# A hybrid decode step on one core: the page table by one small load, and the sample group's attention ordered behind the first unit of the prompt's

## The chip, the cores and the metric

The kernel runs on one core of a Trainium2 chip. The metric is the device time of one execution in microseconds (us), the median of several executions. The engines are named as in the profile: PE is TensorE (its weight loads, PEld, overlap its matmuls), DVE is VectorE, ACT is ScalarE, POOL is GpSimd and SP is SyncE, which here only issues DMAs. SPq, ACTq and POOLq are the queues on which these engines issue DMAs. Each engine takes its own instructions in the order of the program.

## What is computed

One inference step of a one-layer decoder for two groups that share their weights: a prompt group (1 sequence of 1024 tokens, width 1024) and a sample group (8 sequences, one new token each, with 1024 past tokens in paged caches). Cut to what matters:

```
z        = rmsnorm(x, g_pre) @ w_in          # queries, three pairs of keys and values, gates, z_a, q_b, f_b, i_b, z_b
prompt   : attention over compressed blocks (64), over selected blocks (here all 16 of 64 tokens, causal)
           and over a window of 512; each a softmax with a linear bias of the distance; summed by gates
           HGRN2 recurrence (4 heads, 128 x 128 state) over the 1024 tokens
sample   : full_cmp = concat(cmp_cache[page_table], new)   # page_table (8, 8) int32: 8 pages of 128 tokens per sequence
           full_slc = concat(slc_cache[page_table], new)
           the same three attentions for one query per sequence, and one step of the recurrence
h        = x + rmsnorm(concat(y_a, y_b) @ w_out, g_post)
y        = h + (p @ ple_proj) * sigmoid(h @ ple_gate)
```

The outputs are y for both groups, the new key and value rows, the windows and the recurrent states.

## The kernel before, in words

The whole step is one program of 18918 instructions. Products of float32 data are made of two or three matmuls over a high and a low part (`split`, lines 50 and 51; the weights by lines 238 and 239). Nearly every matmul is issued by the helper `mm` at line 42, so the profile tells matmuls apart by their tiles. The stages follow each other in the program in this order.

1. `consts` and `load_x`: the nine tiles of x come in by SP's queue, are normed and transposed (line 218) into `xhi` and `xlo`. `load_w` (line 225 on) brings a slice of w_in in eight pieces of 128 rows into `w_raw` (3 buffers, line 233); ACT rounds each piece to `w_hi` (line 238) and DVE makes the rest `w_lo` (line 239).
2. `project`: `feat` and `tok` make the projections, one group of columns after the other, between them the recurrence (`hgrn_a`, `hgrn_b`, `hgrn_sample`). Behind the input-gate columns (`tok(C_IB, ...)`, line 335) stands `page_index` (line 336, body 645 to 658). It loads the table with eight DMAs, the i-th of which writes page i of all 8 sequences into each of 16 partitions (16 x 8 numbers), and makes `pidx[16 i + r, b] = 16 * page_table[b, i] + r`, the row numbers by which `gather` (line 660) fetches 128 rows of 8 tokens of a cache with an indirect DMA on POOL's queue. `hgrn_sample` stores its values to `v_d` (line 427) and orders the first of the eight loads behind that store; the other seven have no order.
3. `compress`, then the last projections. While the z_b columns are projected (line 420) the maxima of units 0 and 1 of the prompt's attention are made.
4. `attention` (line 618): the prompt's attention goes by 16 units (8 blocks of 128 queries in the order 5, 6, 7, 4, 3, 2, 1, 0, times 2 key-value heads). A unit is a list of steps: for each 128 keys a block (two score matmuls of 512 columns into a "ph" buffer, exponentials by ACT at line 955 into P, on the diagonal a mask by POOL at lines 958 to 962, four matmuls P times V into a "pb" buffer), the outputs of the three branches, and the store at line 995. Between the blocks of unit i stand the maxima of unit i + 2 (scores into a "pa" buffer, reductions by DVE at lines 909 to 918, the joined reduction at line 923, and `aux`, line 931, which turns the maxima by matmuls into a row of the query tile). Unit 1's maxima end with the same two steps. "ph" and "pb" have 2 buffers each in PSUM, "pa" 3, "pt" 1.
5. Beside this runs `side_work`, a generator that is advanced once every second step: `sample_attention` (line 1000) and then `finish_setup`, which loads and splits w_out. `sample_attention` sets up (query matrices Qb, Qp and Qr from small loads; masks and distances by memsets and iotas on POOL; compressed attention), then goes through the 8 sequences four times with a `yield` at each: twice over the cached selected keys, once over the window's, and once over all values. Per sequence a gather into "sg" (3 buffers), transposes at line 1125 into "pa", a split into two of the four "KT" buffers, and two products with Qr into "pt". The new keys and values `kvs` (line 1022) also take a "KT" buffer for a while.
6. `finish`: w_out, the second norm, the gate products and the outputs.

The order of the instructions on each engine is not that of the text. A planner orders them by a priority and a simulated timeline. Inside `high_priority(offset=0)` the units' steps all start from one priority, and the side work's instructions, under `high_priority(offset=600)`, come 600 ahead of it. `after(ins, first)` (line 45) adds an edge for the planner alone: `ins` is placed behind `first`, with no semaphore between them on the chip.

Of the kernel before, what the change touches and what calls it, by code (L numbers as in the profile page):

```python
# [19 lines left out]
T = 1024  # L20
# [7 lines left out]
class Kernel:  # L28
# [195 lines left out]
    def load_w(self, src, *parts):  # L224
# [4 lines left out]
        for k in range(8):  # L229
            raw = self.wpool.tile([128, 512], F32, name="w_raw", bufs=3)[:, :width]  # L230
            o = 0
            for c0, n in parts:
                dma = nc.sync.dma_start(raw[:, o:o + n], src[k * 128:(k + 1) * 128, c0:c0 + n])
                o += n
            hi = self.wpool.tile([128, 512], F32R, name="w_hi", bufs=9)[:, :width]
            lo = self.wpool.tile([128, 512], F32R, name="w_lo", bufs=9)[:, :width]
            g = self.gpre[:, k:k + 1]
            nc.scalar.activation(hi, raw, AF.Copy, scale=g)  # L238
            nc.vector.scalar_tensor_tensor(lo, raw, g, hi.bitcast(F32), op0=OP.mult, op1=OP.subtract)  # L239
            out.append((hi, lo))  # L240
# [377 lines left out]
    def attention(self, ctx):  # L618
# [3 lines left out]
        for i, u in enumerate(units):  # L622
# [3 lines left out]
            for j, f in enumerate(blocks):  # L626
                with self.tc.high_priority(offset=0):
                    f()
                while done < len(steps) * (j + 1) // len(blocks):
                    with self.tc.high_priority(offset=0):  # L630
                        steps[done]()
                    done += 1
                n += 1
                if n % 2 == 0:
                    with self.tc.high_priority(offset=600):
                        next(side, None)
# [8 lines left out]
    def page_index(self, pool):  # L645

        nc = self.nc
        pt = self.a["page_table"]
        raw = pool.tile([128, NB], I32, name="pt_raw", bufs=1)
        for i in range(8):  # L650
            dma = nc.sync.dma_start(raw[16 * i:16 * i + 16], bass.AP(tensor=pt.tensor, offset=pt.offset + i, ap=[[0, 16], [8, NB]]))
            if i == 0:
                self.pidma = dma
        lane = pool.tile([128, NB], I32, name="pt_lane", bufs=1)
        nc.gpsimd.iota(lane, pattern=[[0, NB]], base=0, channel_multiplier=1)
        nc.vector.tensor_scalar(lane, lane, 15, None, op0=OP.bitwise_and)
        self.pidx = self.cp.tile([128, NB], I32, name="pidx")
        nc.vector.scalar_tensor_tensor(self.pidx, raw, 16.0, lane, op0=OP.mult, op1=OP.add)

# [279 lines left out]
    def branches(self, qb, g, i):  # L939
# [4 lines left out]
        for br in (2, 0, 1):  # L944
            k0, k1 = (0, 0) if br == 2 else self.ranges(qb)[br]
            acc = self.ps_b.tile([128, 512], F32, name="pb").rearrange("p (h d) -> p h d", h=4)
            for kb in range(k0, k1 + 1):
                def block(br=br, kb=kb, first=kb == k0, last=kb == k1, acc=acc):
                    n = 8 * qb + 7 if br == 2 else 128
                    ks = slice(kb * 128, kb * 128 + n)  # L950
                    ps = self.ps_h.tile([128, 512], F32, name="ph")[:n].rearrange("p (h q) -> p h q", q=128)
                    self.mm(ps, KA[br, g][:, ks], QA, True, False)
                    self.mm(ps, KB[br, g][:68, ks], QB, False, True)
# [46 lines left out]
    def sample_attention(self, ctx):  # L1000
        nc, a = self.nc, self.a
        sp = self.pool(ctx, "samp", bufs=1, side="right")
        R = 64
        tpt = lambda: self.ps_t.tile([128, 512], F32, name="pt")
        Qb = sp.tile([128, NB, 8], F32, name="Qb")
        nc.gpsimd.memset(Qb, 0.0)
        Qv = Qb.rearrange("p b (g c two) -> p g two c b", g=2, two=2)
        Qs = sp.tile([128, 4, NB], F32, name="Qs")
        Ql = sp.tile([128, 4, NB], F32, name="Ql")
        nc.sync.dma_start(Qs, self.qh_d[:, :, T:].rearrange("c p b -> p c b"))  # L1010
        nc.sync.dma_start(Ql, self.ql_d[:, :, T:].rearrange("c p b -> p c b"))
        nc.vector.tensor_tensor(Qs, Qs, Ql, op=OP.add)
# [3 lines left out]
        Qp = sp.tile([128, NB, R], F32, name="Qp")  # L1016
        nc.gpsimd.memset(Qp, 0.0)
        for h in range(8):
# [3 lines left out]
        kvs = sp.tile([128, 512], F32, name="KT", bufs=4)[:NB]  # L1022
        nc.sync.dma_start(kvs, self.kvs_d[:, 256:])
        pt = tpt()
# [11 lines left out]
        gd = self.dram.tile([NB, 24], F32, name="g_d")  # L1036
        nc.sync.dma_start(gd, self.gs)
        gate = sp.tile([R, 3], F32, name="gate")
        nc.sync.dma_start(gate, gd.rearrange("b (h t) -> (b h) t", t=3))
        li = sp.tile([R, R], I32, name="li")  # L1040
        lj = sp.tile([R, R], I32, name="lj")
        nc.gpsimd.iota(li, pattern=[[0, R]], base=0, channel_multiplier=1)
        nc.gpsimd.iota(lj, pattern=[[1, R]], base=0, channel_multiplier=0)
        sl = sp.tile([R, 1], I32, name="sl")
# [35 lines left out]
        sc = sp.tile([R, 68], F32, name="sc")  # L1080
        nc.gpsimd.memset(sc, 0.0)
        nc.gpsimd.iota(sc[:, :63], pattern=[[16, 63]], base=31 - T, channel_multiplier=0, allow_small_or_imprecise_dtypes=True)
# [14 lines left out]
        bi = sp.tile([R, 16], F32, name="bi")  # L1097
        nc.gpsimd.iota(bi, pattern=[[1, 16]], base=0, channel_multiplier=0, allow_small_or_imprecise_dtypes=True)
        nc.vector.tensor_reduce(ex[:, 0:1], ps, axis=AX.X, op=OP.min)
# [33 lines left out]
        for br in range(2):  # L1133
            nj = 4 if br else 8
            s = sp.tile([R, nj, 128], F32, name=f"s{br}")
            nc.gpsimd.iota(s, pattern=[[1, nj], [nj, 128]], base=-128 * nj, channel_multiplier=0,
                           allow_small_or_imprecise_dtypes=True)
            nc.vector.tensor_scalar(s, s, slope, None, op0=OP.mult)
# [256 lines left out]
```

## Time and profile before

| what | value |
|---|---|
| median of 3 runs | 1088.88 us (1085.47 to 1092.77) |
| the profiled execution | 1086.7 us |
| its span, from first to last instruction | 1085.0 us |
| PE busy | 1047.7 us (97%) |
| DVE, ACT, POOL busy | 617.8, 388.4, 243.9 us |
| mean granted TensorE clock | 0.991 |
| DMA packets | 118815, 116.44 MB |

The profile shows one execution. Times of rows are microseconds from the start of the span unless marked ns. A row of a timeline has start, duration, engine, line, operation, tile written and tile read, shapes, a count, and in brackets how long the engine idled before it and what released it. Matmul durations include a pipelined end, so the distance of two starts is the time that one costs in a row of them. The granted clock is given as a share of full speed: 1.00 is 2.4 GHz, 0.50 is 1.2 GHz.

### The profile page before, as it was taken

The page shows a single profiled execution, that of the slowest core. Times are in us where ns is not written, and L with a number is a line of the kernel's source. Part 1 is how long each engine was busy: PE and PEld are TensorE (multiplying, and loading weights), DVE is VectorE, ACT ScalarE, POOL GpSimd, SP SyncE. Part 2 cuts the span into 40 slices and gives each one's busy share as a digit, 9 for nine tenths or more (in the row PEclk, how much of TensorE's full clock was granted, in tenths as well). Part 3 has the DMA queues.
Part 4 walks back from the last instruction along what each step waited for, and adds up shares of the span by engine and source line. Part 5 has one row for each costly group of instructions (what it writes and reads, how often), then busy time and mean ns, then how long its engine had stood idle before and what let it go on. Part 6 is the DMA issues. An engine that isn't in the chain of part 4 may idle for free.

```text
span 1085.0 us, 18918 instructions
## 1 busy us (share of the span) xinstructions
PE 1047.7 (97%) x7021; PEld 933.6 (86%) x7021; DVE 617.8 (57%) x1822; ACT 388.4 (36%) x786; POOL 243.9 (22%) x276
## 2 busy tenths in 40 slices
PE   4999999999899999999989999999999999999998
PEld 3898799999889899999968888888788888778876
DVE  6847565665494634543665656766665686471223
ACT  4622234313132335432234544553554232241112
POOL 0014232331041133002032211121323133131111
PEclk9999999999989999999989999999999999999999
DMA  6212023323464766403568611001831573121110
GB/s 195 79 29 69 11 72 100 117 89 119 131 176 142 214 210 211 148 1 107 129 215 266 154 29 51 20 21 53 227 106 40 161 209 90 41 97 49 49 35 30
DMA packets 118815, 116.44 MB, mean 107 GB/s; under 512 B 18710, under 2 KB 100974, under 8 KB 116420
## 3 DMA queue, kind: packets, MB, share of 16 engines
q1 hardware_dynamic: 97220, 79.46, 25.7%
q10 hardware_dynamic: 19200, 19.01, 5.1%
q0 software_dynamic: 2304, 16.78, 4.5%
q8 instruction: 55, 0.90, 0.4%
q14 instruction: 36, 0.29, 0.1%
HBM read 84.84 MB, written 29.31 MB: 105 GB/s over the span
## 4 chain that ended last, share of the span: by engine, by line
PE 82%; DMA 9%; DVE 4%; issue 2%; ACT 2%; POOL 1%; SPq 0%; ACTq 0%; DVEq 0%; POOLq 0%
PE pa L42 39%; PE pb L42 26%; PE ph L42 9%; PE pt L42 4%; DMA vb<-v_d 2%; DMA w_raw<-w_in 2%; PE ph L717 1%; PE pa L1125 1%; DMA fw_raw<-w_out 1%; DMA fw_raw<-ple_gate 1%; DMA x_in<-x_prompt 1%; DVE fw_lo L51 1%; PE ph L1319 1%; DMA gpre<-g_pre 0%; DMA f_oa<-oa_d 0%
## 5 line engine op out<-in xcount | busy, mean ns | idle before, releaser
L42 PEld LDWEIGHTS pb<-V,P 128*128 128x128 f32 x1056 | 141.8, 191 | 12.1 <-POOL P L960 1.2
L42 PE MATMUL pb<-V,P 128*128 128x128 f32 x1056 | 148.1, 276 | 0.4 <-DVE mx L909 0.4
L42 PE MATMUL pa<-xhi,w_hi 128*128 128x344 f32 x384 | 126.0, 330 | 2.6 <-ACT w_hi L238 1.1
L42 PE MATMUL pa<-xlo,w_hi 128*128 128x344 f32 x384 | 124.5, 326 | 0.0
L42 PE MATMUL pa<-xhi,w_lo 128*128 128x344 f32 x384 | 123.5, 327 | 0.0
L955 ACT ACTIVATE P<-ph 128x512 f32<-128x512 f32 (+4 forms) x148 | 85.6, 595 | 98.6 <-PE ph L42 69.3
L916 DVE CUSTOM_DVE_ANT_0 junk<-pa,mask 128x320 bf16<-128x320 f32 (+5 forms) x150 | 72.9, 497 | 27.8 <-PE pa L42 26.6
L42 PE MATMUL pa<-w_lo,xhi 128*128 128x256 f32 (+2 forms) x256 | 79.5, 314 | 0.0
L42 PE MATMUL pa<-w_hi,xlo 128*128 128x256 f32 (+2 forms) x256 | 79.2, 314 | 0.0
L42 PE MATMUL pa<-w_hi,xhi 128*128 128x256 f32 (+2 forms) x256 | 78.6, 316 | 0.0
L42 PEld LDWEIGHTS pa<-xhi,w_hi 128*128 128x128 f32 x384 | 73.5, 192 | 4.2 <-ACT w_hi L238 1.7
L238 ACT ACTIVATE w_hi<-w_raw,gpre 128x512 fp32r<-128x512 f32 (+2 forms) x80 | 47.5, 616 | 78.2 <-DMA w_raw<-w_in 43.0
L42 PEld LDWEIGHTS pa<-xlo,w_hi 128*128 128x128 f32 x384 | 73.5, 192 | 0.1
L42 PEld LDWEIGHTS pa<-xhi,w_lo 128*128 128x128 f32 x384 | 73.0, 191 | 0.2
L42 PE MATMUL ph<-QA,KA 128*128 128x512 f32 (+4 forms) x148 | 66.7, 453 | 3.8 <-ACT P L955 2.9
L42 PE MATMUL pa<-KB,QB 65*128 65x320 f32 (+6 forms) x195 | 63.4, 363 | 0.1
L239 DVE SCALAR_TENSOR_TENSOR w_lo<-w_raw,gpre,w_hi 128x512 fp32r<-128x512 f32 (+2 forms) x80 | 50.6, 653 | 21.4 <-ACT w_hi L238 20.7
L42 PE MATMUL pa<-fw_hi,yh 128*128 128x512 f32 (+1 forms) x160 | 61.9, 387 | 0.2 <-ACT fw_hi L50 0.2
L42 PE MATMUL pa<-fw_lo,yh 128*128 128x512 f32 (+1 forms) x160 | 61.6, 385 | 0.0
L42 PE MATMUL pa<-fw_hi,yl 128*128 128x512 f32 (+1 forms) x160 | 61.6, 385 | 0.0
L42 PE MATMUL ph<-QB,KB 68*128 68x512 f32 (+4 forms) x148 | 58.5, 406 | 0.0
L559 POOL TENSOR_TENSOR K<-K,E 128x512 f32<-128x512 f32 x24 | 36.4, 1517 | 94.2 <-PE pb L42 57.2
(457 smaller groups left out, 2411.9 us busy)
## 6 DMA issues: line engine op xcount, KB each, us to landing
w_raw<-w_in SPq DMA_DIRECT2D x32, 256.0 KB
w_raw<-w_in SPq DMA_DIRECT2D x48, 128.0 KB
VS<-sg SPq DMA_DIRECT2D x8, 512.0 KB
sg<-cache_win_kv SPq DMA_DIRECT2D x16, 256.0 KB
fw_raw<-w_out SPq DMA_DIRECT2D x16, 256.0 KB
fw_raw<-ple_gate SPq DMA_DIRECT2D x16, 256.0 KB
f_x<-x_prompt SPq DMA_DIRECT2D x8, 512.0 KB
win_kv_sample<-cache_win_kv SPq DMA_DIRECT2D x8, 511.0 KB
```

Source lines behind the costliest of these rows:

```text
L42: return self.nc.tensor.matmul(out, lhsT, rhs, start=start, stop=stop, skip_group_check=True)
L51: lo_eng.tensor_tensor(lo, src, hi.bitcast(F32), op=OP.subtract)
L238: nc.scalar.activation(hi, raw, AF.Copy, scale=g)
L239: nc.vector.scalar_tensor_tensor(lo, raw, g, hi.bitcast(F32), op0=OP.mult, op1=OP.subtract)
L559: nc.gpsimd.tensor_tensor(Kv[:, :, 0], Kv[:, :, 0], Ev[:, :, 1:2].to_broadcast([128, nb, m]), op=OP.mult)
L717: nc.tensor.transpose(pt[:, i * 128:(i + 1) * 128], src[b0 + j // 2, kv][:, j % 2, 2 * jp:2 * jp + 2].rearrange("p j d -> p (j d)"), self. ...
L916: nc.vector.tensor_tensor_reduce(junk, pm, mk, 1.0, -1e30, op0=OP.add, op1=OP.max, accum_out=o)
L955: nc.scalar.activation(P, ps, AF.Exp, scale=0.125)
L1125: nc.tensor.transpose(pt[:, j * 128:(j + 1) * 128], rows(j), self.ident)
L1319: nc.tensor.transpose(pt[:, c], h[:, k * 128:(k + 1) * 128], self.ident[:n, :n])
```

## The change

`page_index` loads the 64 numbers of the table once, as 8 partitions (pages) by 8 columns (sequences), behind the last weight load of the input-gate columns and, as before, behind the store to `v_d`. They are copied to floats, and one matmul with a 0/1 matrix of 8 by 128 (made by POOL with a memset and two selects) writes page i to the 16 partitions of its group in a "pt" buffer, from where DVE forms `pidx`. In `attention` the side work isn't advanced while the steps of unit 0 are written (`if i and ...`), so its first call comes with the second step of unit 1, and the instructions of the sample group's setup that have no inputs or only loaded ones are ordered behind `self.anchor`, the first score matmul of the block written last, here that of unit 1's first block. The later iota for the window's distances takes the anchor of its own time.

```diff
@@ load_w
-                dma = nc.sync.dma_start(raw[:, o:o + n], src[k * 128:(k + 1) * 128, c0:c0 + n])
+                dma = self.lastw = nc.sync.dma_start(raw[:, o:o + n], src[k * 128:(k + 1) * 128, c0:c0 + n])
@@ attention
-                if n % 2 == 0:
+                if i and n % 2 == 0:
                     with self.tc.high_priority(offset=600):
                         next(side, None)
@@ page_index
-        raw = pool.tile([128, NB], I32, name="pt_raw", bufs=1)
-        for i in range(8):
-            dma = nc.sync.dma_start(raw[16 * i:16 * i + 16], bass.AP(tensor=pt.tensor, offset=pt.offset + i, ap=[[0, 16], [8, NB]]))
-            if i == 0:
-                self.pidma = dma
+        raw = pool.tile([8, NB], I32, name="pt_raw", bufs=1)
+        self.pidma = nc.sync.dma_start(raw, bass.AP(tensor=pt.tensor, offset=pt.offset, ap=[[1, 8], [8, NB]]))
+        self.after(self.pidma, self.lastw)
+        num = pool.tile([8, NB], F32, name="pt_num", bufs=1)
+        nc.vector.tensor_copy(num, raw)
+
+        sel = self.zpool.tile([128, 688], F32, name="z_s", bufs=2)[:8, :128]
+        nc.gpsimd.memset(sel, 1.0)
+        nc.gpsimd.affine_select(sel, sel, pattern=[[1, 128]], compare_op=OP.is_ge, fill=0.0, base=0, channel_multiplier=-16)
+        nc.gpsimd.affine_select(sel, sel, pattern=[[-1, 128]], compare_op=OP.is_ge, fill=0.0, base=15, channel_multiplier=16)
         lane = pool.tile([128, NB], I32, name="pt_lane", bufs=1)
         nc.gpsimd.iota(lane, pattern=[[0, NB]], base=0, channel_multiplier=1)
         nc.vector.tensor_scalar(lane, lane, 15, None, op0=OP.bitwise_and)
+        lf = pool.tile([128, NB], F32, name="pt_lf", bufs=1)
+        nc.vector.tensor_copy(lf, lane)
+        p = self.ps_t.tile([128, 512], F32, name="pt")[:, :NB]
+        self.mm(p, sel, num, True, True)
         self.pidx = self.cp.tile([128, NB], I32, name="pidx")
-        nc.vector.scalar_tensor_tensor(self.pidx, raw, 16.0, lane, op0=OP.mult, op1=OP.add)
+        nc.vector.scalar_tensor_tensor(self.pidx, p, 16.0, lf, op0=OP.mult, op1=OP.add)
@@ branches, block
-                    self.mm(ps, KA[br, g][:, ks], QA, True, False)
+                    self.anchor = self.mm(ps, KA[br, g][:, ks], QA, True, False)
@@ sample_attention
+        gated = lambda x: self.after(x, self.anchor)
-        nc.gpsimd.memset(Qb, 0.0)
+        gated(nc.gpsimd.memset(Qb, 0.0))
-        nc.sync.dma_start(Qs, self.qh_d[:, :, T:].rearrange("c p b -> p c b"))
+        gated(nc.sync.dma_start(Qs, self.qh_d[:, :, T:].rearrange("c p b -> p c b")))
...
```

`gated` goes in the same way around the load of Ql, the memset of Qp, the loads of kvs and of the gates (`gd`), the iotas `li`, `lj`, `bi` and `s`, and the memset of `sc`. The gathers, their transposes, the split into "KT" and everything that has computed inputs carry no such edge of their own.

## Rows read from the trace of the kernel before

**Rows 1.** The page's first part: span, and PE's busy time, share and instructions.
```profile
span 1085.0 us, 18918 instructions
...
PE 1047.7 (97%) x7021; PEld 933.6 (86%) x7021; DVE 617.8 (57%) x1822; ACT 388.4 (36%) x786; POOL 243.9 (22%) x276
```
**Rows 2.** The page's chain that ended last, shares of the span by engine.
```profile
PE 82%; DMA 9%; DVE 4%; issue 2%; ACT 2%; POOL 1%; SPq 0%; ACTq 0%; DVEq 0%; POOLq 0%
```
**Rows 3.** Timeline of SP's queue, first 60 us: start, duration, queue, line, transfer, count.
```profile
16.85 3.27 SPq L651 DMA_DIRECT2D pt_raw<-page_table  x7
20.24 17.45 SPq L233 DMA_DIRECT2D w_raw<-w_in  x14
```
**Rows 4.** Table of stretches at the start: length, busy time per engine, PEclk, DMA share, GB/s.
```profile
24.00:26.00 2.00, 2.00 (x8) 2.00 (x8) 0.00 (x0) 0.00 (x0) 0.00 (x0) 1.00 0.05 1
...
27.04:39.84 12.80, 11.24 (x72) 10.14 (x71) 10.55 (x41) 10.04 (x18) 1.44 (x1) 1.00 0.58 168
45.00:50.00 5.00, 5.00 (x36) 4.96 (x36) 4.36 (x16) 1.98 (x4) 0.00 (x0) 1.00 0.01 2
```
**Rows 5.** Chain that ended last, in order of time, first 62 us: start, duration, what.
```profile
20.64 7.24 DMA w_raw<-w_in
...
29.86 2.26 DMA w_raw<-w_in
```
**Rows 6.** Timeline of ACT, first 58 us.
```profile
27.96 0.72 ACT L238 ACTIVATE w_hi<-w_raw,gpre 128x512 fp32r<-128x512 f32 x1 [6.01 <-DMA w_raw<-w_in]
```
**Rows 7.** Table of stretches at the passage into attention (PE, PEld, DVE, ACT, POOL).
```profile
546.00:549.00 3.00, 1.31 (x5) 0.56 (x5) 2.91 (x13) 1.87 (x2) 2.39 (x4) 1.00 0.82 195
549.00:552.33 3.33, 1.68 (x5) 0.79 (x4) 3.21 (x9) 0.60 (x1) 2.74 (x9) 0.50 0.98 395
552.33:559.26 6.93, 6.93 (x26) 5.58 (x27) 5.77 (x29) 4.07 (x7) 0.27 (x2) 0.50 1.06 345
```
**Rows 8.** Waits from 546 to 553: engine, line, releaser, us, times, longest.
```profile
PEld pa L42 <- POOL P L958: 2.3, 1, 2.3
PE pa L42 <- DVE Mp L923: 1.7, 1, 1.7
```
**Rows 9.** Line 1015: durations in ns (minimum, median, maximum), first and last start.
```profile
L1015 DVE TENSOR_SCALAR Qb<-Qs x4: 179/492/2000, 548.7 to 551.8; 64x16 f32<-64x16 f32 x4
```
**Rows 10.** Timeline of DVE, 526 to 582.
```profile
551.99 0.19 DVE L923 TENSOR_REDUCE Mp<-mx 128x12 fp32r<-128x36 f32 x1
```
**Rows 11.** Timeline of POOL, 545 to 553.
```profile
547.56 0.95 POOL L662 DMA_INDIRECT sg<-cache_slc_kv,pidx  x1 [0.30 <-issue]
...
550.08 1.04 POOL L1136 IOTA s<- 64x1024 f32 x1
551.05 0.66 POOL L958 TENSOR_SCALAR_AFFINE_SELECT P<-P 47x512 f32<-47x512 f32 x1
```
**Rows 12.** Timeline of SP's queue, 139 to 141.
```profile
140.20 0.34 SPq L651 DMA_DIRECT2D pt_raw<-page_table  x1
```
**Rows 13.** Timeline of DVE, 143 to 145.
```profile
144.18 0.16 DVE L658 SCALAR_TENSOR_TENSOR pidx<-pt_raw,pt_lane 128x8 int32<-128x8 int32 x1
```
**Rows 14.** Timeline of PE, 576 to 584.
```profile
577.31 0.48 PE L42 MATMUL ph<-QA,KA 128*47 128x512 f32 x1
...
580.56 1.17 PE L42 MATMUL pt<-KT,Qr 128*128 128x512 f32 x4
```
**Rows 15.** The tile fw_raw: its loads from w_out, first and last start.
```profile
L1228 SPq DMA_DIRECT2D fw_raw<-w_out x16: 327/346/536, 754.8 to 793.6; - x16
```
**Rows 16.** The tile fw_hi: its first product.
```profile
L42 PE MATMUL pa<-fw_hi,yh x160: 277/394/503, 848.2 to 1079.9; 128*128 128x512 f32 x144, 128*128 128x256 f32 x16
```
**Rows 17.** Table of stretches, the time of w_out's loads.
```profile
770.00:800.00 30.00, 27.48 (x188) 23.55 (x187) 19.55 (x77) 16.40 (x30) 7.50 (x11) 1.00 0.54 159
```
**Rows 18.** Timeline of ACT, 555 to 600: splits into KT.
```profile
567.10 0.59 ACT L50 CAST KT<-pa 128x512 fp32r<-128x512 f32 x1 [0.23 <-PE pa L1125]
...
581.07 1.07 ACT L50 CAST KT<-pa 128x512 fp32r<-128x512 f32 x2 [0.76 <-PE pt L42]
```

More of the change, by code (lines that the diff above doesn't have):

```diff
@@ L1009, in sample_attention @@
         Ql = sp.tile([128, 4, NB], F32, name="Ql")
-        nc.sync.dma_start(Qs, self.qh_d[:, :, T:].rearrange("c p b -> p c b"))
-        nc.sync.dma_start(Ql, self.ql_d[:, :, T:].rearrange("c p b -> p c b"))
+        gated(nc.sync.dma_start(Qs, self.qh_d[:, :, T:].rearrange("c p b -> p c b")))
+        gated(nc.sync.dma_start(Ql, self.ql_d[:, :, T:].rearrange("c p b -> p c b")))
         nc.vector.tensor_tensor(Qs, Qs, Ql, op=OP.add)
@@ L1016, in sample_attention @@
         Qp = sp.tile([128, NB, R], F32, name="Qp")
-        nc.gpsimd.memset(Qp, 0.0)
+        gated(nc.gpsimd.memset(Qp, 0.0))
         for h in range(8):
@@ L1022, in sample_attention @@
         kvs = sp.tile([128, 512], F32, name="KT", bufs=4)[:NB]
-        nc.sync.dma_start(kvs, self.kvs_d[:, 256:])
+        gated(nc.sync.dma_start(kvs, self.kvs_d[:, 256:]))
         pt = tpt()
@@ L1036, in sample_attention @@
         gd = self.dram.tile([NB, 24], F32, name="g_d")
-        nc.sync.dma_start(gd, self.gs)
+        gated(nc.sync.dma_start(gd, self.gs))
         gate = sp.tile([R, 3], F32, name="gate")
@@ L1041, in sample_attention @@
         lj = sp.tile([R, R], I32, name="lj")
-        nc.gpsimd.iota(li, pattern=[[0, R]], base=0, channel_multiplier=1)
-        nc.gpsimd.iota(lj, pattern=[[1, R]], base=0, channel_multiplier=0)
+        gated(nc.gpsimd.iota(li, pattern=[[0, R]], base=0, channel_multiplier=1))
+        gated(nc.gpsimd.iota(lj, pattern=[[1, R]], base=0, channel_multiplier=0))
         sl = sp.tile([R, 1], I32, name="sl")
@@ L1080, in sample_attention @@
         sc = sp.tile([R, 68], F32, name="sc")
-        nc.gpsimd.memset(sc, 0.0)
+        gated(nc.gpsimd.memset(sc, 0.0))
         nc.gpsimd.iota(sc[:, :63], pattern=[[16, 63]], base=31 - T, channel_multiplier=0, allow_small_or_imprecise_dtypes=True)
@@ L1097, in sample_attention @@
         bi = sp.tile([R, 16], F32, name="bi")
-        nc.gpsimd.iota(bi, pattern=[[1, 16]], base=0, channel_multiplier=0, allow_small_or_imprecise_dtypes=True)
+        gated(nc.gpsimd.iota(bi, pattern=[[1, 16]], base=0, channel_multiplier=0, allow_small_or_imprecise_dtypes=True))
         nc.vector.tensor_reduce(ex[:, 0:1], ps, axis=AX.X, op=OP.min)
@@ L1135, in sample_attention @@
             s = sp.tile([R, nj, 128], F32, name=f"s{br}")
-            nc.gpsimd.iota(s, pattern=[[1, nj], [nj, 128]], base=-128 * nj, channel_multiplier=0,
-                           allow_small_or_imprecise_dtypes=True)
+            gated(nc.gpsimd.iota(s, pattern=[[1, nj], [nj, 128]], base=-128 * nj, channel_multiplier=0,
+                                 allow_small_or_imprecise_dtypes=True))
             nc.vector.tensor_scalar(s, s, slope, None, op0=OP.mult)
```

## Prediction

> **What bounds the kernel.** I read the shares of the span by engine first, then the chain that ended last, then tables of stretches to find where TensorE is not at its pace, and last the timelines of the other engines in those stretches. TensorE is busy 1047.7 of 1085.0 us [rows 1], and the chain runs through it for 82% [rows 2]. A change can therefore give back only the 37 us in which TensorE idles and the stretches in which it runs below its pace. No matmul of weight goes away here, so the question is whether the two edits sit beside such a place. Both do.
>
> First place, the start. Seven of the eight page table loads are issued at 16.85 to 20.12 on SP's queue, just ahead of the weight loads from 20.24 on [rows 3]. From 24 to 26 us the queues move 1 GB/s with 0.05 of their engines busy [rows 4], and the same holds for all of 18 to 26. The weight load issued at about 20.5 lands 7.24 us later; one of the same kind soon after takes 2.26 [rows 5]. ScalarE, which rounds the weights in order, stands still for 6.01 us behind it [rows 6]. TensorE feels less of that, since it works off earlier weights for most of the time. Between 27.04 and 39.84 it starts 72 matmuls in 12.80 us, and in the steady stretch 45 to 50 it starts 36 in 5.00 [rows 4]. At 5.00/36 = 0.139 us each the 72 are worth 10.0 us, so 2.8 us were lost.
>
> Second place, the passage into attention. Between 546 and 549 us TensorE is busy 1.31 of 3.00. From 549 to 552.33 it is busy 1.68 of 3.33 at a granted clock of 0.50 (the lower level, 1.2 GHz), and from 552.33 to 559.26 it is busy throughout, still at 0.50 [rows 7]. The waits that end there are the reduced maxima of unit 1 on VectorE (1.7 us) and the mask on the first probabilities on GpSimd (2.3 us, on the weight side) [rows 8]. Both sit behind the sample group's setup: the four Qb copies on VectorE fill 548.7 to 552.0, with 179, 492 and 2000 ns as minimum, median and maximum [rows 9], and the maxima's last reduction comes right after, at 551.99 [rows 10]. GpSimd does three gathers, the last from 547.56 to 548.5, then memsets and iotas, the longest from 550.08 to 551.1, and only then the mask, at 551.05 [rows 11].
>
> **The change, part by part.** Page table, removed: 7 loads of 128 numbers. SP spends 3.27 us issuing them [rows 3], which costs little by itself, since the next weight load also waited for its buffer until about 20.1. Their gain is that the fourth weight slice lands about 5 us sooner (7.24 against 2.26 [rows 5]). ScalarE's 6.01 us of standing shrink to about 1, and TensorE stops running dry after 27. Of the 2.8 us lost I take 2.4, because not every gap in those 12.80 us need come from the load. Bounds: 0 and 2.8. A loss I exclude here: nothing is added to this queue before 137.
>
> The Trainium skill speaks against this term ("DMA: Bandwidth & Descriptors", section "Anatomy of one DMA"): it says that descriptor generation is a small, variable part, so that many descriptors can be issued before their cost shows. By that rule 896 numbers would be nearly free and the sum would lose its 2.4 us. The trace disagrees: eight microseconds at 1 GB/s follow the seven loads [rows 4].
>
> Page table, added: one load of 64 numbers behind the last input-gate weight load and the v_d store (before, one load of 128 numbers stood at 140.20 [rows 12]); a copy to floats on VectorE; three small GpSimd instructions and one iota with no inputs, which can run while GpSimd is idle early; one float copy of the lane; one matmul with 8 rows and 8 columns; the final combination, now out of PSUM. The VectorE parts have the size of the 158 ns combination at 144.18 [rows 13], together 0.3 us, beside a TensorE that has projections to do. The matmul itself is under 0.3 us. The new risk is its place: it waits for the load and the copy, and TensorE's next projections stand behind it in order. If it were placed as soon as the load is issued, the wait would be a load's 2.3 us [rows 5]; before, the combination came 4 us after the issue and did not wait. Bounds 0.1 and 2.6; I take 0.3. VectorE would hold the decayed queries behind the same copy; that is inside the 2.6.
>
> Attention: the generator's first eight calls move from unit 0 to unit 1, and the memsets, iotas and small loads of the setup are ordered behind unit 1's first score matmul (at 577.31 before [rows 14]). What goes: the Qb copies and the iotas between the maxima and TensorE. The last reduction of unit 1 can then start at about 548.7 instead of 551.99, the mask at about 548.8 instead of 551.05 (an estimate: the gathers, which carry no such order, still end at 548.5, and the instructions between are setup). TensorE has scores, probabilities times values and the maxima of unit 2 to do, so I expect no break there. What is late next: before 549 TensorE waits for VectorE's backlog of early maxima and for ScalarE's first exponentials, and this 1.69 us of idling (3.00 − 1.31 [rows 7]) stays, and with it, I assume, the fall of the clock. So of the stretch at the lower level I keep the 6.93 us in which TensorE is busy throughout and strike the 3.33 us before them; the 1.68 us of matmuls in these still have to be done, at full speed in the end, 1.68 × 0.5 = 0.84. The gain is 3.33 − 0.84 = 2.5. Bounds: 0, if TensorE finds nothing to do before 552 either, and 6.0, if the clock doesn't fall: then the work of the whole 10.26 us, (1.68 + 6.93) × 0.5 = 4.3, takes 4.3.
>
> What the moved setup costs at its new place: all its instructions and its SP loads come in again about one unit later, among unit 1's and 2's maxima. VectorE stood 3.25 us for four copies that take 0.18 each at best, 2.5 us more. TensorE then has more blocks in hand than at 549, so I charge 0.3, between 0 and 2.5. The sample group's end and the w_out loads (754.8 to 793.6 [rows 15]) slide by some 20 us, to about 814, still ahead of the first product with them at 848.2 [rows 16]; the 2.5 us of idling from 770 to 800 [rows 17] slide along, at no charge either way.
>
> Sum: −2.4 + 0.3 − 2.5 + 0.3 = −4.3 us. The profiled execution took 1086.7 (span 1085.0 and 1.7 around it), which gives 1082.4; it lies 2.2 under the median 1088.9 of the runs shown, so against that I forecast **1084.6**.
>
> **Rivals.** (B) Both places heal entirely: the clock stays up, and the end of w_out's loading no longer holds ScalarE. Then −2.8 − 6.0 − 2.5 + 0.6 = −10.7, 1078.2. For it: the waits of [rows 8] are all setup. Against: the idling before 549 is not touched by the edits.
>
> (C) The stall only moves. The four Qb copies and GpSimd's iotas stay neighbours, so VectorE stands again in front of maxima that TensorE needs, at half clock again. The second term becomes 0 and the charge 2.5: −2.4 + 0.3 + 2.5 = +0.4, 1089.3. For it: the same instructions run in the same order. Against: in unit 1 more blocks are ready.
>
> The Trainium skill bears on C ("SBUF — State Buffer", section "Who interferes with whom"): VectorE copies of this kind and GpSimd share a port pair, and whichever issues second is blocked for the whole instruction. The spread 179 to 2000 ns agrees [rows 9]; by that rule the block of 3.25 us comes along to the new place.
>
> (D) Slower: held PSUM buffers. Gathers and key transposes of the sample group are not ordered behind the anchor; the kvs load, which shares the four KT buffers with the split keys, and Qr are. Before, the second sequence's split ran at 567.10 and the third only at 581.07 [rows 18], after the first product with Qr at 580.56 [rows 14]. With the setup some 20 us later, transposed keys can sit in up to three "pa" buffers, the only ones that maxima of unit 2 use. Some 16 maxima at about 0.65 us on VectorE are 10 us that would start late; TensorE runs dry for up to 10 us and then has the lower clock as long as in the last row of [rows 7], 6.93 × 0.5 = 3.5. Then −2.4 + 0.3 + 13.5 = +11.4, 1100.3. It decides once the buffers stay held past the last block of unit 1. Against: before, with one buffer held for 14 us, TensorE did not idle there.
>
> **Chances.** Forecast 0.52 (own range 1080 to 1089), B 0.18, C 0.18, D 0.12 with most of D's outcomes only partly as bad. Instructions are ordered by a planner, so a shift of a few microseconds elsewhere rides on each. A difference of 1% is about what a measurement of this kernel can tell from none: 10.9 us, so faster means under 1078.0 and slower over 1099.8. B reaches the first in somewhat under half of its cases, and a few of the forecast's do: faster 0.15. D reaches the second in half of its cases: slower 0.07. Within 1%: 0.78. The range, 1076 to 1094, leaves out the best of B and the worst of D.
>
> **What would show it.** Right: no stretch at 1 GB/s after 18 us, ScalarE's 6.01 us gone, some 80 matmuls in 27 to 40; a page load near 140 with no wait over 0.5 us at its matmul; the last reduction of unit 1 within 1 us of its maxima, the half clock rising near 556; the Qb copies around 565 to 580. Wrong: weight loads that still land after 7 us, a granted clock of 0.50 for 10 us or more, TensorE waiting for maxima of unit 2 in "pa" (D), or the gained microseconds idled away at w_out's loads.

## The result and the profile after

The changed kernel takes 1096.07 us (median of 19 runs, 1088.94 to 1104.76), the kernel before, run beside it, 1088.5 (19 runs). The ratio is 1.0071, with a 95% interval of 1.0046 to 1.0095: slower by about 7.6 us, where 4 us less were forecast. It is still within 1%, but the sign is wrong and the time is above the range.

The page's first part and its chain by engine, after (answering to [rows 1, 2]):

```profile
span 1098.1 us, 18889 instructions
...
PE 1059.1 (96%) x7023; PEld 945.9 (86%) x7023; DVE 614.0 (56%) x1824; ACT 389.7 (35%) x786; POOL 241.3 (22%) x279
...
PE 86%; DMA 7%; DVE 3%; issue 1%; ACT 1%; POOL 1%; SPq 0%; DVEq 0%; ACTq 0%; POOLq 0%
```

This execution took 1099.9 us, 3.8 over the median. PE has two more instructions and is busy 11.4 us longer, at a mean granted clock of 0.978 instead of 0.991, so the stretches have to be read with their granted clock.

**The start** (table of stretches, timeline of ACT) went as forecast:

```profile
24.00:26.00 2.00, 2.00 (x12) 2.00 (x11) 1.69 (x5) 0.73 (x1) 0.00 (x0) 1.00 0.60 157
27.04:39.84 12.80, 12.80 (x89) 12.75 (x88) 11.34 (x48) 10.15 (x19) 2.47 (x3) 1.00 0.33 86
```
```profile
21.57 0.72 ACT L238 ACTIVATE w_hi<-w_raw,gpre 128x512 fp32r<-128x512 f32 x1 [0.31 <-DMA w_raw<-w_in]
...
24.67 0.73 ACT L238 ACTIVATE w_hi<-w_raw,gpre 128x512 fp32r<-128x512 f32 x1 [0.91 <-DMA w_raw<-w_in]
```

The gap at 1 GB/s of [rows 4] is filled, ScalarE's 6.01 us of [rows 6] in front of the fourth slice are 0.31 (0.91 is the longest of its next waits for these loads), and 89 matmuls instead of 72 start in the 12.80 us. The table's one load, its product and the combination (SP's queue, PE, DVE) cost nothing visible; the product has no wait in front of it:

```profile
136.13 0.29 SPq L650 DMA_DIRECT2D pt_raw<-page_table  x1
...
142.96 0.38 PE L42 MATMUL pt<-pt_num,z_s 8*128 8x8 f32 x2
...
143.68 0.16 DVE L667 SCALAR_TENSOR_TENSOR pidx<-pt,pt_lf 128x8 int32<-128x8 f32 x1
```

**The passage into attention** (stretches; DVE; POOL; the Qb copies; answering to [rows 7, 9, 10, 11]):

```profile
543.00:547.17 4.17, 2.71 (x11) 1.40 (x10) 3.59 (x16) 2.14 (x3) 3.25 (x4) 1.00 0.61 175
547.17:557.41 10.24, 10.24 (x40) 8.48 (x39) 3.40 (x13) 2.97 (x5) 0.24 (x2) 0.50 1.03 350
```
```profile
546.44 0.19 DVE L932 TENSOR_REDUCE Mp<-mx 128x12 fp32r<-128x36 f32 x1
```
```profile
546.70 0.64 POOL L967 TENSOR_SCALAR_AFFINE_SELECT P<-P 47x512 f32<-47x512 f32 x1 [0.31 <-DVE Mp L932]
...
567.46 1.02 POOL L1146 IOTA s<- 64x1024 f32 x1
```
```profile
L1025 DVE TENSOR_SCALAR Qb<-Qs x4: 167/178/577, 569.7 to 570.8; 64x16 f32<-64x16 f32 x4
```

Unit 1's joined reduction comes 5.6 us earlier (some 2 of them because the whole kernel is ahead there: its first score matmul starts at 545.23 instead of 547.33), TensorE no longer waits in the stretch at half clock, and the Qb copies take 0.18 us in the median. But the half clock lasts as long as before, 10.24 us.

**The late part** is where the time went. Each row of a table of stretches tells two losses: idling is the length less PE's busy time; and since a stretch at 0.50 does half the work of one at 1.00, the clock costs the length times (1 − PEclk). Before, then after:

```profile
740.00:800.00 60.00, 57.48 (x401) 49.52 (x400) 39.73 (x160) 28.79 (x51) 17.01 (x24) 1.00 0.56 156
800.00:885.00 85.00, 84.88 (x523) 72.31 (x521) 54.17 (x242) 31.47 (x59) 25.51 (x34) 1.00 0.42 121
```
```profile
740.00:800.00 60.00, 58.69 (x387) 50.80 (x387) 38.23 (x157) 24.27 (x42) 13.17 (x21) 0.86 0.34 98
800.00:885.00 85.00, 81.41 (x499) 69.46 (x498) 51.21 (x228) 33.75 (x62) 23.73 (x33) 0.94 0.44 130
```

Before, 2.5 + 0.1 us of idling and no low clock: 2.6. After, 1.3 + 3.6 of idling and 60 × 0.14 + 85 × 0.06 = 13.5 of clock: 18.4, or 16 more. The whole attention, from its first score matmul to its last store (871.6, before 857.6), takes 326.4 us instead of 310.3, 16 more as well, and the whole span grew by 13.1.

What stands at 769 is the end of the sample group. Its outputs are copied to the tile o8, one copy for each of the 8 sequences. The last o8 copy came 20.9 us later than before (763.2 instead of 742.3), and then these rows follow (PE; SP's queue; ACT; stretches):

```profile
766.24 1.95 PE L42 MATMUL pt<-two,o 16*128 16x8 f32 x16
```
```profile
768.98 0.33 SPq L1004 DMA_DIRECT2D oa_d<-og  x1
```
```profile
769.75 0.60 ACT L964 ACTIVATE P<-ph 128x512 f32<-128x512 f32 x1 [3.04 <-PE ph L42]
...
777.87 0.60 ACT L964 ACTIVATE P<-ph 128x512 f32<-128x512 f32 x1 [4.67 <-PE ph L42]
```
```profile
766.00:769.04 3.04, 3.04 (x24) 2.82 (x23) 2.13 (x12) 0.60 (x1) 1.46 (x2) 1.00 0.00 0
769.04:779.28 10.24, 10.24 (x38) 8.73 (x38) 4.59 (x21) 1.79 (x3) 0.77 (x2) 0.50 0.21 66
779.28:789.50 10.22, 10.22 (x73) 9.22 (x73) 6.35 (x28) 5.21 (x10) 1.30 (x2) 1.00 0.50 133
```

Eight narrow products (16 instructions, 8 columns each) add up the sample's heads just before unit 7's store (units count from 0). 2.8 us after their start the clock falls to 0.50 for 10.24 us: 38 matmuls start in them, and 73 in the next 10.22. ScalarE stands still in front of scores. The clock falls again for 6.8, 6.8 and 3.4 us at 793, 824 and 861. The first of w_out's loads starts at 769.5 and the last at 822.5, 53 us instead of the 39 of [rows 15], and the first product with them slides from the 848.2 of [rows 16] to 859.0.

### The profile page after: what moved, and what is told of

It is laid out like the page before. It is cut to its first block, busy times and chain, and to the rows that moved or that the text cites. A ratio compares the mean times of both kernels' runs of the same rounds, so it can differ in the third digit from the quotient of the medians.

```text
span 1098.1 us, 18889 instructions
## 1 busy us (share of the span) xinstructions
PE 1059.1 (96%) x7023; PEld 945.9 (86%) x7023; DVE 614.0 (56%) x1824; ACT 389.7 (35%) x786; POOL 241.3 (22%) x279
## 4 chain that ended last, share of the span: by engine, by line
PE 86%; DMA 7%; DVE 3%; issue 1%; ACT 1%; POOL 1%; SPq 0%; DVEq 0%; ACTq 0%; POOLq 0%
PE pa L42 39%; PE pb L42 29%; PE ph L42 9%; PE pt L42 4%; DMA vb<-v_d 2%; DMA w1r<-cmp_w 2%; PE ph L726 1%; PE pa L1135 1%; DMA w_raw<-w_in 1%; PE ph L1329 1%; PE ph L218 1%; DMA cg<-cache_cmp_kv,pidx 1%; DMA V<-x_prompt 1%; DMA QB<-qh_d 0%; DMA fw_raw<-w_out 0%
## 5 line engine op out<-in xcount | busy, mean ns | idle before, releaser
L42 PEld LDWEIGHTS pb<-V,P 128*128 128x128 f32 x1056 | 150.6, 201 | 13.4 <-PE ph L42 1.0
L42 PE MATMUL pb<-V,P 128*128 128x128 f32 x1056 | 156.9, 286 | 0.6 <-DVE pb L988 0.6
L42 PE MATMUL pa<-KB,QB 65*128 65x320 f32 (+6 forms) x195 | 65.9, 373 | 1.8 <-DMA QB<-qh_d 1.3
L42 PE MATMUL pb<-x,w1h 128*128 128x384 f32 (+1 forms) x192 | 55.9, 353 | 1.4 <-ACT x L50 1.4
```

Of the source, the lines that this page charges most:

```text
L42: return self.nc.tensor.matmul(out, lhsT, rhs, start=start, stop=stop, skip_group_check=True)
```

## The experiments

A "call" below is one advance of the side work's generator; the change leaves out the eight calls of unit 0. All times are medians, all ratios against the kernel before on the same chip, with 95% intervals. Three theories stood at first: the late end of the sample group costs; the planner re-sorts the tail whatever is changed; the page edit's gain is lost in the compression stage.

**1. The page edit alone** (the old `attention` and `sample_attention`).

> Late slide (my theory: the ordering of the sample group behind the first unit ends that group some 20 us later, w_out's loads then run beside the last eight units and TensorE's clock falls there): without the attention edits the w_out loads stay at 755 to 795, no half clock between 765 and 870; about 1084 to 1086, 2 to 4 us under the kernel before (ratio 0.996 to 0.998). Any reordering does it (rival: the planner re-sorts the tail for whatever change): half clock behind 765 here too, 1090 to 1097. Given back in the compression stage (second rival: the 3.9 us won by 150 are lost to ScalarE's waits for w1r between 405 and 440): equal to before, 1088, with milestones 3 to 4 us ahead at 390 and 1 or less at 440.

Measured: 1084.95 us, 0.9962 (0.9940 to 0.9983). Run once more in the last series:

> The page edit alone: 0.994 to 0.998 again, 2 to 4 us under the kernel before, whichever theory of the passage holds.

Measured: 1084.06, 0.9977 (0.9952 to 1.0003). The page edit is worth 2.5 to 4 us (the second interval reaches 1). Behind 765 the two profiles show 3.4 and 6.8 us of half clock, not none as expected, but no loss like that of the changed kernel; the page edit doesn't re-sort the tail (see 6 to 9). Of the compression stage: in 405 to 440 PE idled 2.85 us in the first of these profiles and 0.62 in the second (before 0.5, the changed kernel 3.25). So that loss comes and goes with the same kernel, and it isn't the answer; experiment 2 idles nothing there and is as slow as the changed kernel.

**2. The attention edits alone.**

```diff
-        raw = pool.tile([8, NB], I32, name="pt_raw", bufs=1)
...
+        raw = pool.tile([128, NB], I32, name="pt_raw", bufs=1)
+        for i in range(8):
+            dma = nc.sync.dma_start(raw[16 * i:16 * i + 16], bass.AP(tensor=pt.tensor, offset=pt.offset + i, ap=[[0, 16], [8, NB]]))
...
+        nc.vector.scalar_tensor_tensor(self.pidx, raw, 16.0, lane, op0=OP.mult, op1=OP.add)
```

> Late slide: all of the loss is in the attention edits, so with the old page table the time is that of the changed kernel or the 2 to 4 us more that the page edit gives: 1096 to 1100 (ratio 1.007 to 1.011), half clock at least twice between 765 and 870, w_out loads over 50 us instead of 39. Any reordering: anything between 1085 and 1097. Page edit as the cause: 1086 to 1089.

Measured: 1099.58, 1.0100 (1.0067 to 1.0133), with half clock four times between 770 and 863. All of the loss is in the attention edits.

**3. The calls of unit 0 again, with the new order behind the anchor; 4. the calls left out, without the order.**

```diff
-                if i and n % 2 == 0:
+                if n % 2 == 0:
```
```diff
-        gated = lambda x: self.after(x, self.anchor)
+        gated = lambda x: x
```

> The generator is called in unit 0 again, the order behind the anchor (now a score matmul of unit 0) stays. If the eight skipped calls make the slide: the sample group's end goes back by most of 20 us, w_out loads at 755 to 800, time 1083 to 1088. If the order behind the anchor makes it: as the changed kernel, 1094 to 1098.

> The calls begin in unit 1, no order behind the anchor. If the skipped calls make the slide: as the changed kernel, 1094 to 1098, setup at 555 to 570. If the order behind the anchor makes it: setup near 548 as before, 1083 to 1088.

Measured: 1087.11, 0.9980 (0.9958 to 1.0002), and 1097.87, 1.0075 (1.0047 to 1.0103). The skipped calls make the slide (last o8 at 740.2 and 767.7) and the loss; the order behind the anchor moves the setup (Qb at 559.0 and 546.8) and costs nothing that these runs can tell. I had expected the skip to move the setup as well; it doesn't.

**5. The changed kernel, with the eight calls made good in unit 1.**

```diff
-                if i and n % 2 == 0:
+                if i == 1 or i and n % 2 == 0:
```

> The changed kernel, its eight skipped calls made good in unit 1 (a call after every step there). If the late end of the sample group is what costs: last o8 back to 740 to 745, w_out loads from 754 to 800, less than 8 us of half clock behind 560, ratio 0.994 to 0.999 (1083 to 1088). If leaving unit 0 without the group is what costs: ratio 1.005 to 1.011 as for the changed kernel.

Measured: 1083.59, 0.9943 (0.9914 to 0.9972), last o8 at 736.1. Beside the page edit on one chip:

> If the passage is worth its 2.2 us: ratio 0.993 to 0.996 and 2 us or more under the page edit run beside it. If not: 0.995 to 0.999 and within 1 us of it.

Measured: 1081.89, 0.9944 (0.9918 to 0.9970), 2.2 us under the page edit. Unit 0 without the side work does no harm; only the calls that are missing later do. The late part of this second run (740 to 800, 800 to 885), beside that of the changed kernel above:

```profile
740.00:800.00 60.00, 55.91 (x370) 47.88 (x369) 40.39 (x170) 28.80 (x52) 18.31 (x25) 0.97 0.59 159
800.00:885.00 85.00, 85.00 (x513) 72.58 (x513) 56.65 (x228) 31.80 (x61) 26.11 (x31) 1.00 0.40 122
```

4.1 us of idling and 1.8 of clock (3.3 and 3.6 in the first run). This kernel is faster than the one before and the changed one.

**6 to 9. The dose:** four calls skipped, eight calls ahead, the calls of unit 3 left out (nine, since that unit has 17 steps), twelve skipped; each on the page edit, without the order; the four lines below in this order.

```diff
-                if n % 2 == 0:
+                if n > 8 and n % 2 == 0:
+                if not i or n % 2 == 0:
+                if i != 3 and n % 2 == 0:
+                if n > 24 and n % 2 == 0:
```

> New page table, no order behind an anchor, only the first four calls skipped. If lateness costs by its amount: last o8 near 755, ratio about half way between 0.996 and 1.0075, 1.000 to 1.004. If the cost hangs on where the group's last narrow products fall among the units, not on the amount: anything from 0.994 to 1.010, and the half clock begins 3 to 5 us behind those products.

> New page table, no anchor, a call after every step of unit 0, so the group is eight calls ahead. If lateness costs by its amount: last o8 near 722, w_out loads before 780, ratio 0.990 to 0.996. If only the place among the units decides: 0.994 to 1.010. If VectorE's backlog before the first unit grows with the calls: TensorE idles more between 546 and 600 and the ratio is over 1.

> New page table, no anchor, unit 0 as before, but no calls in unit 3: the passage into attention is that of the page edit alone and only the group's last part and w_out slide. If the late end costs: last o8 near 760, half clock of 15 us or more between 765 and 870, ratio 1.004 to 1.011. If it is the passage that costs: 0.994 to 0.999.

> New page table, no anchor, the first twelve calls skipped. If lateness costs by its amount: later than the kernel with eight skipped, ratio 1.011 to 1.018 with last o8 behind 775. If it costs because the group's end products fall on the seam of two units (2.7 us ahead of a unit's last store in all four slow kernels, in the middle of a unit in the fast ones): last o8 near 775 in the middle of unit 8, no more than 3.5 us of half clock right behind it, ratio 0.998 to 1.006.

| calls | last o8, us | ratio |
|---|---|---|
| 8 ahead | 720.5 | 1.0020 (1.0001 to 1.0039) |
| as before (experiment 1) | 744.3 | 0.9962 (0.9940 to 0.9983) |
| 4 skipped | 758.9 | 1.0102 (1.0076 to 1.0128) |
| pause in unit 3 (9 calls) | 759.1 | 1.0057 (1.0034 to 1.0080) |
| 8 skipped (experiment 4) | 767.7 | 1.0075 (1.0047 to 1.0103) |
| 12 skipped | 780.9 | 1.0179 (1.0137 to 1.0222) |

The pause has the passage of the page edit and only the late slide, and it is slow: the late end costs by itself. But the time doesn't follow the amount. To be early gains nothing, and four skipped calls cost as much as eight. Where the clock falls differs. In the four kernels with a last o8 at 759 to 768 whose narrow products stand 2.7 us ahead of unit 7's store (the changed kernel and experiments 2, 4 and 8), the half clock behind the products lasts 6.8 or 10.24 us. In the first profiles of experiments 1, 3 and 5, with the products in the middle of unit 6, it lasts 3.4 us, and in that before there is none, nor in the second of experiment 1, though that is the same program as the first. Four skipped calls put the products behind a store, with 3.4 us; but there another serial piece of the group, its softmax on VectorE, falls on the seam of units 4 and 5 (the end of one and the start of the next), where TensorE waits for the joined maxima. PE and the stretches of that kernel:

```profile
685.26 0.22 PE L42 MATMUL pa<-ident,Mp 128*4 128x128 f32 x1 [1.64 <-DVE Mp L932]
```
```profile
684.00:686.66 2.66, 1.01 (x7) 0.68 (x7) 2.30 (x14) 0.91 (x4) 0.85 (x2) 1.00 0.00 0
686.66:690.00 3.34, 3.34 (x12) 2.40 (x12) 2.45 (x14) 1.45 (x4) 0.63 (x1) 0.50 0.12 39
...
700.30:703.73 3.43, 3.43 (x21) 3.24 (x19) 2.07 (x6) 1.83 (x3) 0.00 (x0) 0.50 0.02 5
```

1.65 us of idling there were followed by 17.07 us at half clock. The theory that the seam alone decides fell with the twelve calls: their products stand in the middle of unit 8, with 3.4 us of half clock behind them as expected of it, and the kernel is the slowest of all. It loses elsewhere (690 to 740, 740 to 800, 800 to 885):

```profile
690.00:740.00 50.00, 49.96 (x360) 43.58 (x361) 30.06 (x116) 22.40 (x41) 8.98 (x13) 0.93 0.07 20
740.00:800.00 60.00, 60.00 (x464) 52.04 (x463) 39.60 (x164) 25.57 (x46) 10.24 (x18) 0.97 0.11 29
800.00:885.00 85.00, 79.49 (x478) 66.67 (x477) 50.43 (x237) 35.68 (x65) 24.63 (x34) 0.92 0.61 172
```

There is one more difference, the order of the matmuls themselves. The last 1640 that PE starts, from about unit 7's store on, come in one order, matmul for matmul, in the kernel before and in experiments 1, 3 and 5, and in another, again one and the same, in the changed kernel and experiments 2, 4 and 8 (401 of the 1640 places differ, none of the last 989). So the slow kernels of these share the place of the narrow products and also a different order of the last units, and these runs don't tell the two apart.

**10 and 13. The narrow products left out,** in the changed kernel and in the page edit.

```diff
-        for b in range(NB):
-            self.mm(po[:, b * 8:(b + 1) * 8], o8[:, b], two, True, True)
+        self.mm(po[:, :R], o8[:, 0], self.ident[:16, :R], True, True)
```

> The changed kernel with one product of 64 columns in place of the eight of 8 columns that add up the sample group's heads (the sample's attention output is no longer the sum of its two halves, and only of sample 0). If these narrow products bring the clock down at 769: no half clock between 765 and 780, 5 to 7 us gained, ratio 1.000 to 1.003. If the seam does it, whatever product stands there: half clock still from about 768, ratio 1.005 to 1.007.

> The page edit alone, with one product of 64 columns in place of the eight of 8 columns (the sample's attention output is left incomplete). If the narrow products cost only on the seam: 1.3 us of products and 1.7 of half clock, ratio 0.992 to 0.996. If they cost 8 us wherever they stand: 0.987 to 0.990, and the distance to the changed kernel without them stays 11 us.

Measured: 1087.94, 0.9998 (0.9967 to 1.0029), and 1085.07, 0.9973 (0.9940 to 1.0005). The changed kernel gains 0.0073, 8 us (about 4 either way by the two intervals), and the page edit nothing that can be told; both forecasts for it were lower. The eight products take 1.95 us in either kernel. But the cut takes away more than them: up to the products PE's order is that of the changed kernel, behind them the last units' matmuls come in yet another order, as they do in all of experiments 10 to 16. So the 8 us are what the products and the order that comes with them cost together. The late part of the changed kernel without them:

```profile
740.00:800.00 60.00, 58.08 (x403) 50.18 (x401) 37.39 (x161) 26.15 (x46) 16.38 (x24) 0.91 0.42 119
800.00:885.00 85.00, 83.53 (x500) 70.82 (x500) 56.43 (x236) 34.52 (x66) 25.47 (x32) 0.98 0.49 145
```

1.9 + 1.5 us of idling and 7.1 of clock, 10.5 instead of 18.4. The half clock at 769 is gone, but there is another from 781.5 to 791.7. Over all profiles: in 12 of the 15 with the eight products the clock falls within 2.6 us of their end (not in that before, in experiment 12 and in the second of experiment 1), and in none of the five without them (10, 13 to 16) within 18 us. What is left between the two kernels without the products, 0.0025, is within the intervals.

**14 to 16. The sum kept, by two products of 32 columns** (o8, set to zero first, laid on four groups of partitions), on the page edit, the changed and the caught-up kernel.

```diff
-            nc.vector.tensor_copy(o8[:, b], po)
+            nc.vector.tensor_copy(o8[32 * (b % 4):32 * (b % 4) + 16, b // 4], po)
...
+        for i in range(2):
+            self.mm(po[:, 32 * i:32 * i + 32], o8[:, i], two, True, True)
```

> The page edit, and the sample's heads added by two products of 32 columns out of o8 laid on four groups of partitions. Seam theory: as the page edit or a little less, 0.992 to 0.997.

> The changed kernel with the two products of 32 columns. If the eight narrow products on the seam bring the clock down: ratio 0.998 to 1.002, as without them, and no half clock between 765 and 780. If lateness as such costs: 1.005 to 1.008.

> The changed kernel with the calls made good in unit 1, and the two products. If the passage is worth its 2 us once the end is not late: 2 to 4 us under the page edit with the two products, ratio 0.989 to 0.994. If not: equal to it.

Measured: 0.9988 (0.9961 to 1.0015), 1.0027 (0.9993 to 1.0060), 0.9989 (0.9959 to 1.0018). The changed kernel gets 0.0044 back, hardly more than the two intervals allow, and lands between the two forecasts; its profile has no half clock from 560 to 794, but it is of the second fastest of the 12 executions (1082.84, median 1090.17). The two others get nothing, their point estimates are 0.0011 to 0.0046 worse than without the edit. The caught-up kernel lies level with the page edit, not 2 to 4 us under it.

**11 and 12. One slice of w_out loaded,** in the changed kernel and in the page edit.

```diff
-            self.wo.update(self.load_fw(a["w_out"][0], k // 8, (k % 8,), "fw", 16))
+            if k == 0:
+                self.wo.update(self.load_fw(a["w_out"][0], 0, (0,), "fw", 16))
+            self.wo[k // 8, k % 8] = self.wo[0, 0]
```

> The changed kernel with one of the sixteen w_out slices loaded and split, used for all (the output projection is that of one slice). If w_out's loads beside the short units cost: no half clock and no idling over 1 us between 785 and 880, ratio under 1.000, 1083 to 1089. If the group's end alone costs: 1.003 to 1.007.

> The same cut in the kernel with the page edit alone: what w_out's loads cost where they begin at 758. It idles 3.2 us between 740 and 800 for them and has 1.7 us of half clock: ratio 0.990 to 0.994, 1078 to 1082. If the two kernels with one slice stand as far apart as those with sixteen (11 to 12 us), w_out isn't the cause; under 6 us apart, it is half of it or more.

Measured: 1096.12, 1.0078 (1.0048 to 1.0108), and 1086.40, 0.9987 (0.9955 to 1.0018). They stand 0.0091 apart, with all slices 0.0109. My first theory, that the slide hurts because w_out's loads then run beside the short units, is wrong: without them the changed kernel is as slow. From its first score matmul to its last store attention is 7.1 us shorter in the changed kernel, and 10.2 or 5.8 in the page edit, which has two profiles. Both lose most of it again behind the last store: from there to the end the changed kernel takes 235.0 us instead of 226.5, the page edit 234.0 instead of 227.8. Behind 885 they idle 6.4 and 5.3 us and lose 3.4 us to the clock; between 870 and 940 ScalarE waits 18.1 and 17.1 us for the loads of ple_gate. So the loads are not free, but their cost is much the same with and without the slide. The 12.3 us that ScalarE waits for w_out's loads in the changed kernel (14.2 before) were no gain to take by this cut.

## Why the prediction was wrong

**Page table, removed (−2.4) and added (+0.3): right.** 2.1 us were forecast and 2.5 to 4.1 measured by the two runs. Without the seven loads the weight loads flow at 157 GB/s from 24 to 26 where they stood at 1. The eight microseconds at 1 GB/s were six: from 18 to 20 the queues moved 12 GB/s, and 7 after the change. The Trainium skill did not speak against this term: "DMA: Bandwidth & Descriptors", section "Anatomy of one DMA", says that many descriptors can be emitted before their added cost shows, but of the path on which GpSimd issues a DMA. These loads were issued by SP, so no run here tests that sentence.

**The passage (−2.5): the mechanism right, the size near. The moved setup (+0.3): too small.** In the profile of the changed kernel PE's idling from 540 to 600 falls from 3.35 to 1.46 us, 1.9 less, and without the kernel's lead the reduction comes 3.5 us earlier, where 3.3 were forecast. The half clock did not shorten from 10.24 us to the 6.93 that the sum kept (so B fell). PE idles nowhere from 547 to 600, but from 600 to 690 it idles 2.40 us instead of 0.38: 2.0 for the moved setup and the later calls, within the bounds of 0 to 2.5, and as much as the passage had won. In the caught-up kernel it is 0.98. That kernel lies 2.2 us under the page edit beside it, where 2.2 were forecast, in ratio 0.0033 there and 0.0019 in the first series, but level with it in the pair with two products; all these intervals overlap, so a gain of that size isn't shown by the times. Rival C's second half didn't come at this place: the iota of 1.02 us held up only small mask arithmetic, and the copies took 0.18 us in the median. Nor did D, with no idling from 547 to 600. One thing was not foreseen: in the nine profiles with the order behind the anchor the half clock of the passage lasts 6.8 to 10.24 us in all, in the eleven without it 10.24 in five and 17 to 20 in six. Of the signs of being wrong that were named, one came: 10.24 us at 0.50, at the passage and again at 769.

**"Slide by some 20 us ... at no charge either way": this step failed.** The slide was sized rightly, 20.9 us. The charge is 12 us (experiment 4 against experiment 1, 0.0113) or 14 (the changed kernel against the caught-up one, 0.0128). I looked at the end of w_out's loads and its slack before the first product, and in that I wasn't wrong: in experiments 11 and 12, with fifteen of the loads taken away, the two kernels stand 0.0091 apart instead of 0.0109. What I took no price for was the work of the group itself. I had counted its end by its last load, not by its narrow products, and had charged clock only to idling. Where it now ends the clock falls behind its narrow products, and 10.24 us at half clock alone cost 5.1: 38 matmuls start instead of 73. Leaving the products out, with the new order that comes of it, gives back 8 us (experiments 10 and 13). The other 4 to 6 us of the charge have no place yet.

In all the attention edits were forecast at −2.2 us, and they cost 10 to 12: the changed kernel stands 0.0094 or 0.0109 over the page edit.

**What stays open.** That skipping the calls costs 12 to 14 us is shown by skipping them, giving them back and making them good. That the clock falls behind the narrow products is shown by 12 of 15 profiles against none of five. How the charge divides between these products and the other order of the last units is not shown: every edit that took the products away changed the order too. An edit that keeps the order and changes the products alone, or the reverse, was not run. Why the clock stays down for 10.24 us in one place and 3.4 in another isn't: the seam of two units goes with the long stretches in four kernels, but the changed kernel without the products has a stretch of 10.24 us all the same, 12 us later, and twelve skipped calls cost 18 parts in 1000 without a long one there. Nor was it settled why eight calls ahead gain nothing.

## What to carry to other kernels

Work that fills another stage's gaps has a place, not only a length: if it is moved, price its own serial and narrow pieces at their new neighbours, not only the last deadline behind it. Where a planner orders the instructions, compare the order of the stage that is filled as well: moving the filler changed it here. A slide "into slack" isn't free on a TensorE that is busy 97% of the time, since the clock can take more than the wait did. When a generator's start is put off, keep its rate: here one line that makes the skipped calls good turned +0.7% into −0.6%.

## What the runs showed of the hardware

The granted clock fell to 0.50 while the profile shows PE busy without a break, 0.9 us behind 16 instructions of 8 columns; no idling marks such a place in the trace, only the clock column and the count of matmuls do. A break of 1.64 us was followed by 17.07 us at half clock. To take away fifteen of the sixteen loads for which ScalarE waits 12 us gained nothing in the time of the kernel; to take away 1.95 us of small products, with the order that came of it, gained 8.

VectorE was held beside GpSimd again at the new place. Two rows of DVE's timeline in the changed kernel:

```profile
567.69 0.84 DVE L1060 TENSOR_SCALAR lj<-lj 64x64 int32<-64x64 int32 x1
567.80 0.73 DVE L1056 TENSOR_SCALAR sl<-sl 64x1 int32<-64x1 int32 x1
```

They have 64 elements per partition and one, and both end at 568.53, just behind the iota of 567.46, shown above, which ends at 568.48; in the kernel before, with no such iota beside them, they took 0.18 and 0.14 us. The second may only have stood behind the first. The Trainium skill states this as an exclusive lock of a shared port ("SBUF — State Buffer", section "Who interferes with whom"); the trace agrees, with 0.84 us for the first of them.
